# Scores from 16-bit pairs: rotated queries and keys of a two-layer decoder kept as two halves in 16 bits

## The chip, the cores and the metric

The kernel runs on one core of a Trainium2 chip. TensorE (PE in the profile) multiplies matrices into eight PSUM banks; VectorE (DVE), ScalarE (ACT) and GpSimd (POOL) work on tiles of 128 partitions in SBUF and on the banks; SyncE (SP) issues all DMA transfers. The metric is device time in microseconds, the median of the runs shown; lower is better.

## The reference, cut to what matters

Two decoder layers on x of 1024 tokens by 1024 features in float32. The part that the change touches is how scores of rotated queries and keys become softmax weights:

```
h = rms_norm(x, attn_norm[layer])
q, k = apply_rope(h @ Wq, cos, sin), apply_rope(h @ Wk, cos, sin)     # heads of 64 features
s = einsum(q, k) * 64**-0.5                                            # float32, masked
p = exp(s - max(s)) ; o = (p @ v) / sum(p)
```

Layer 0 has 8 heads of sparse attention, each in three branches (over compressed keys, selected blocks and a window of 512) and 8 heads with a window of 128 and a sink; with 1024 tokens the selected blocks are all blocks, so that branch is causal attention. Layer 1 has 16 heads of three dilated windows. After each attention comes an output projection, and after that a gated feed-forward block of 2816 hidden units.

## The kernel before, in words

**Numbers.** No large 32-bit product is made in one piece. An operand x is split into a high half h (x rounded to a shorter type) and a low half l = x - h, and a product is hh + lh + hl, three matmuls. Feed-forward weights and activations are split into two float16 halves under a power of two (lines 553 to 635, `splits`, `high`, `lows`). Projections, and rotated queries and keys, use the 32-bit type fp32r: the halves of a projection weight are two such tiles, and so are those of q and k.

**Where q and k come from.** `rope_job` (line 929) multiplies a group of four heads, `evac` takes the two banks out with the cosine and sine tables, and `fin` subtracts and adds the two parts, copies the result to a high tile on ACT, subtracts it from the result on DVE or POOL (`vg` chooses, line 412), and stores both tiles to DRAM with four DMAs. `apart` writes a second copy with every fourth token together for layer 1's far branch. `bk_job` does the same for one pair of keys. Compressed keys come from `cmp_tail`.

**Scores.** A branch loads its q and k (`load_q`, `load_k`, lines 1469 and 1479) as stacks: the 128 contraction rows are 64 features of the high and 64 of the low half of k, against the high half of q twice; a second matmul of 65 or 66 rows adds the high half of k times the low half of q and a row that subtracts the maximum. `s_issue` makes scores with the tokens on the partitions into a bank pS, `maxima` takes row maxima on DVE, TensorE transposes them, ACT copies them and a DMA writes them into that row. `st_unit` makes the transposed scores into a bank pT, at most 512 columns a unit; DVE adds masks, ACT takes the exponential (`weights`), the weights are split into two float16 halves, and `pv_unit` multiplies them with V into pO. In layer 1's second half a head has a far branch (G: two units of eight matmuls of 128 columns) and a near one (N).

**Order.** Five stages of dense jobs (projections, output projections, feed-forward, of one half of the tokens at a time) run in a fixed sequence; the attention of one half runs beside the dense jobs of another. At build time a list scheduler (`run`, line 377) simulates the engines with its own table of costs (`account`, line 295) and puts the instructions of all tasks into one fixed order per engine; on the chip each engine follows its order and waits on semaphores. A task may issue once a tile of its arena is free: S4 has 36 tiles of 4 KB per partition, S2 has 17 of 2 KB. Nearly all instructions are issued through one wrapper, so the profile shows them at one line, L242, and is read by tiles.

Of the kernel before, what the change touches and what calls it, by code (L numbers as in the profile page):

```python
# [10 lines left out]
F32 = mybir.dt.float32  # L11
# [24 lines left out]
FLOOR = -1.0e20  # L36
# [7 lines left out]
N4 = 36  # L44
N2 = 17
# [105 lines left out]
class W:  # L151


    def __init__(self, load, views=None):
        self.load, self.views = load, views
        self.st = self.h = self.l = None
        self.ok = self.split_ = False

# [100 lines left out]
class Kernel:  # L259
    def __init__(self, nc, tc, ctx, io):  # L260
# [15 lines left out]
        self.MR = arena("MR", 20, [P, HB], F32R)  # L276
        self.SM = arena("SM", NSM, [P, 8], F32)
        self.NM = arena("NM", 3, [HB, P], F32R)
# [16 lines left out]
    def account(self, key, name, a, kw):  # L295
# [14 lines left out]
        if key == "s":  # L310
            n = int(np.prod(a[0].shape)) * 4
# [108 lines left out]
    def constants(self):  # L420
# [10 lines left out]
        nc.vector.memset(self.ones, 1.0)  # L431
        self.onesR = c.tile([P, 2], F32R, name="onesr", tag="onesr")
# [13 lines left out]
    def more_constants(self):  # L446
# [8 lines left out]
        yield "v"  # L455
        nc.vector.tensor_scalar(self.sinks8, self.sinks, 1.0 / SCALE, None, op0=ALU.mult)
# [18 lines left out]
    def rows(self):  # L475
        nc = self.nc
        zero, one = self.S4.take(F32), self.S4.take(F32)
        nc.gpsimd.memset(zero.w[0:16], 0.0)
        nc.gpsimd.memset(one.w[0:16], -1.0)
        kh, ql = self.s0["k"][0], self.s0["q"][1]  # L480
        for r in range(2):
            yield "s"
            for i in (0, 4):
                self.dma(ql.some(i, 4)[64 + r], zero.w[0:4])
            for k0, set_ in ((0, r == 0), (2, r == 1), (4, r == 0)):
                if k0 < 4 or r == 0:
                    yield "s"
                    self.dma(kh.some(k0, 2)[64 + r], (one if set_ else zero).w[0:2])
        yield "s"
        for i in range(0, 16, 4):  # L490
            self.dma(self.s1["k"][0].some(i, 4)[64], one.w[0:4])
            self.dma(self.s4["k"][0].some(i, 4)[64], one.w[0:4])
        zero.drop()
        one.drop()
# [58 lines left out]
    def splits(self):  # L553
        for i, w in enumerate(self.wreq):
# [21 lines left out]
            else:  # L576
                w.l = self.S4.take()
                for h, l, s in w.parts():
                    self.nc.scalar.copy(h, s)
                w.split_ = True  # L580
            self.wsp = i + 1

# [346 lines left out]
    def rope_job(self, wt, cols_, n, h, outs, again=None):  # L929
# [4 lines left out]
        def run(*ws):  # L934
# [24 lines left out]
            def fin(kind, dst, head, a, b):  # L959
# [14 lines left out]
                store(dst, head, hb, lb)  # L974
# [3 lines left out]
            def store(dst, head, hb, lb):  # L978
                for z in range(2):
                    for d, b in zip(dst, (hb, lb)):  # L980
                        self.dma(d.some(head, 4)[z * 32:(z + 1) * 32, :, cs].rearrange("c h t -> (c h) t"), f(b.x[:, z]))
                hb.drop()
                lb.drop()
# [1728 lines left out]
```

## Time and profile before

| | |
|---|---|
| Median of three runs | 2691.47 us (2690.44 to 2698.56) |
| The profiled execution's own time | 2696.28 us |
| Span from its first to its last instruction | 2694.6 us |
| TensorE busy | 2548.9 us, 95% of the span |
| DVE, ACT, POOL busy | 1906.2, 1377.9, 779.2 us |
| Mean granted TensorE clock | 0.97 |
| DMA | 394.55 MB, 146 GB/s on average |

Busy time is when an instruction of the engine is running; for TensorE the ends of matmuls are modelled, so a cost per matmul is better read from one start to the next. In the names of tiles S is SBUF (both arenas), PH a tile of softmax weights, pS, pT, pO and pD are PSUM banks (scores for maxima, transposed scores, outputs of attention, dense products), MR row maxima, NM their transposed copy, SM small columns.

### The profile page before, as it was taken

The page shows a single profiled execution, that of the slowest core. Times are in us where ns is not written, and L with a number is a line of the kernel's source. Part 1 is how long each engine was busy: PE and PEld are TensorE (multiplying, and loading weights), DVE is VectorE, ACT ScalarE, POOL GpSimd, SP SyncE. Part 2 cuts the span into 40 slices and gives each one's busy share as a digit, 9 for nine tenths or more (in the row PEclk, how much of TensorE's full clock was granted, in tenths as well). Part 3 has the DMA queues.
Part 4 walks back from the last instruction along what each step waited for, and adds up shares of the span by engine and source line. Part 5 has one row for each costly group of instructions (what it writes and reads, how often), then busy time and mean ns, then how long its engine had stood idle before and what let it go on. Part 6 is the DMA issues. An engine that isn't in the chain of part 4 may idle for free. (4 is left out here: it accounts for less than half of the span.)

```text
span 2694.6 us, 42662 instructions
## 1 busy us (share of the span) xinstructions
PE 2548.9 (95%) x15462; PEld 1691.7 (63%) x15462; DVE 1906.2 (71%) x4270; ACT 1377.9 (51%) x2338; POOL 779.2 (29%) x538
## 2 busy tenths in 40 slices
PE   8878889999999999999999998998999999999998
PEld 7667668655555687765555687775555557754445
DVE  6988877877778776586666577677668885655554
ACT  6455545666666564353444465444556665443332
POOL 4545534211111347650000346533001114500002
PEclk9989989999999999999999999988899999999999
DMA  8655575333343245854444456995547664633320
GB/s 232 214 153 136 153 228 163 87 91 91 87 105 102 91 145 193 258 145 118 114 122 122 126 172 201 281 248 144 144 132 185 172 156 139 193 110 102 102 71 32
DMA packets 457367, 394.55 MB, mean 146 GB/s; under 512 B 53990, under 2 KB 383654, under 8 KB 457156
## 3 DMA queue, kind: packets, MB, share of 16 engines
q1 hardware_dynamic: 457156, 391.82, 50.9%
q8 instruction: 122, 2.00, 0.3%
q14 instruction: 89, 0.73, 0.1%
HBM read 311.43 MB, written 75.85 MB: 144 GB/s over the span
## 5 line engine op out<-in xcount | busy, mean ns | idle before, releaser
L242 PE MATMUL pD<-S,S 128*128 128x512 f16 (+3 forms) x9648 | 2180.7, 379 | 16.3 <-DVE S L242 11.4
L242 PEld LDWEIGHTS <-S 128*128 128x128 f16 x5376 | 511.4, 100 | 585.1 <-issue 35.6
L242 PEld LDWEIGHTS pD<-S,S 128*128 128x128 f32 x4272 | 734.5, 193 | 142.2 <-DVE S L242 8.8
L242 POOL TENSOR_TENSOR S<-S,S 128x1024 fp32r<-128x1024 f32 (+3 forms) x304 | 565.6, 1877 | 817.0 <-ACT S L242 662.1
L242 ACT CAST S<-S 128x512 fp32r<-128x512 f32 (+2 forms) x307 | 298.8, 1027 | 165.6 <-DVE S L242 72.8
L242 DVE SCALAR_TENSOR_TENSOR S<-S,wsc,S 128x1024 f16<-128x1024 f32 x224 | 295.3, 1319 | 60.8 <-ACT S L242 58.0
L242 ACT ACTIVATE S<-pT 128x512 f32<-128x512 f32 (+3 forms) x304 | 170.7, 565 | 297.9 <-DVE pT L242 252.6
L242 ACT ACTIVATE S<-S 128x1024 f16<-128x1024 f32 (+3 forms) x267 | 210.0, 787 | 158.4 <-DVE S L242 149.1
L242 ACT ACTIVATE S<-S,wsc 128x1024 f16<-128x1024 f32 x224 | 253.2, 1142 | 55.7 <-DVE wsc L242 50.0
L242 DVE TENSOR_TENSOR S<-S,S 128x512 fp32r<-128x512 f32 (+4 forms) x162 | 224.2, 1395 | 70.9 <-ACT S L242 63.7
L242 DVE SCALAR_TENSOR_TENSOR S<-pD,SM,S 128x512 f32<-128x512 f32 x208 | 156.2, 751 | 153.0 <-PE pD L242 143.6
L242 PE MATMUL pT<-S,S 128*128 128x128 f32 (+11 forms) x1072 | 226.0, 337 | 16.0 <-ACT S L242 12.9
L242 DVE TENSOR_TENSOR S<-pD,S 128x512 f32<-128x512 f32 (+1 forms) x238 | 156.7, 666 | 111.9 <-PE pD L242 96.5
L242 DVE TENSOR_TENSOR PH<-S,PH 128x512 f16<-128x512 f32 (+2 forms) x236 | 186.7, 796 | 39.8 <-ACT PH L242 37.9
L242 POOL TENSOR_TENSOR PH<-S,PH 128x512 f16<-128x512 f32 (+3 forms) x68 | 83.3, 1225 | 453.7 <-ACT PH L242 388.4
L242 PEld LDWEIGHTS pT<-S,S 128*128 128x128 f32 (+2 forms) x1072 | 173.2, 200 | 44.6 <-ACT S L242 18.0
L242 ACT ACTIVATE S<-pD,SM 128x512 f32<-128x512 f32 (+2 forms) x136 | 80.6, 604 | 210.6 <-PE pD L242 185.7
L242 ACT CAST PH<-S 128x512 f16<-128x512 f32 (+3 forms) x304 | 176.6, 588 | 13.4 <-PE pO L242 6.7
L242 PEld LDWEIGHTS <-PH 128*128 128x128 f16 (+1 forms) x3384 | 128.5, 101 | 72.6 <-DVE PH L242 24.7
L242 PE MATMUL pO<-S,PH 128*128 128x65 f16 (+1 forms) x3192 | 138.7, 199 | 27.9 <-DVE PH L242 20.8
L242 PE MATMUL pS<-S,S 128*128 128x256 f32 (+4 forms) x460 | 121.3, 352 | 20.4 <-DVE SM L242 12.2
L242 DVE TENSOR_TENSOR pT<-pT,S 128x128 f32<-128x128 f32 (+4 forms) x176 | 91.1, 523 | 50.9 <-PE pT L242 49.3
(175 smaller groups left out, 1798.4 us busy)
## 6 DMA issues: line engine op xcount, KB each, us to landing
S<-in_w_gate_up SPq DMA_DIRECT2D x176, 512.0 KB
S<-in_w_down SPq DMA_DIRECT2D x88, 512.0 KB
S<-in_w_qkv_o SPq DMA_DIRECT2D x48, 512.0 KB
S<-in_w_in_e SPq DMA_DIRECT2D x22, 512.0 KB
xd<-S SPq DMA_DIRECT2D x32, 256.0 KB
S<-dhq SPq DMA_DIRECT2D x64, 128.0 KB
S<-in_w_out_e SPq DMA_DIRECT2D x16, 512.0 KB
S<-xd SPq DMA_DIRECT2D x32, 256.0 KB
```

The lines of the kernel that those rows point to most:

```text
L242: return fn(*a, **kw)
```

## The change

Rotated queries and keys become float16 pairs under a power of two. The power comes from a bound: by Cauchy and Schwarz a projected column is no longer than the norm of the weights times sqrt(1024) times the norm's gain, so ACT squares the projection weights with a running sum (27 tiles, the first time each is loaded), TensorE sums over partitions, and four small DVE operations turn the sum into a power of two (`limited`, `power`). Halves then are h = f16(s x) and l = f16(s x - h), the second always on DVE. The scores carry the product of two such scales, which `joint` turns into factors for the exponential, the sinks and the mask tables; row maxima are kept divided by 32768 in float16. DRAM copies of q and k, the loads, and the tiles are 16-bit: q takes one S2 tile where it took an S4 tile, k one tile where it took two. S4 falls to 33 tiles and S2 rises to 22. The planner's rules stay as they are, with the new types in their place.

```diff
-N4 = 36
-N2 = 17
+N4 = 33
+N2 = 22
...
-        self.MR = arena("MR", 20, [P, HB], F32R)
+        self.MR = arena("MR", 20, [P, HB], F16)
...  splits()
+                if w.limit is not None:
...
+                    self.nc.scalar.activation(w.l.w, f(w.st.w), AF.Square, accum_out=k["acc"].t[:, k["i"]:k["i"] + 1])
+                    k["i"] += 1
+                    if k["i"] == k["n"]:
+                        self.go(self.limited(k), 2)
...
+    def limited(self, k):
+        nc, n = self.nc, k["n"]
+        ps = yield from self.over(k["acc"], n)
+        out, inv = k["t"][:, 0:1], k["t"][:, 1:2]
...
+        nc.vector.tensor_mul(out, out, self.long[k["layer"]])
+        self.power(out, out, inv)
+        self.have[("scale", id(k))] = self.scope
...
+    def joint(self, name, q, k):
...
+        nc.vector.scalar_tensor_tensor(t[:, 0:1], q["t"][:, 1:2], SCALE, k["t"][:, 1:2], op0=ALU.mult, op1=ALU.mult)
+        nc.vector.tensor_scalar(t[:, 1:2], t[:, 0:1], STEP, None, op0=ALU.mult)
+        nc.vector.tensor_scalar(t[:, 2:3], t[:, 0:1], -STEP, None, op0=ALU.mult)
+        nc.vector.tensor_mul(t[:, 3:4], q["t"][:, 0:1], k["t"][:, 0:1])
...  rope_job(), fin()
-                yield "a", self.room(S4=2)
-                hb, lb = self.S4.take(), self.S4.take()
-                nc.scalar.copy(hb.w, f(a.w))
-                yield "vg"
-                self.vg(1024, self.o.slack).tensor_sub(lb.w, f(a.w), f(hb.w))
+                yield "a", lambda: max(self.S4.when(), self.have.get(("scale", id(lim)), INF))
+                t = self.S4.take()
...
+                nc.scalar.activation(t.f16(1024), f(a.w), AF.Copy, scale=lim["s"])
+                yield "v"
+                nc.vector.scalar_tensor_tensor(t.f16(2048)[:, 1024:2048], f(a.w), lim["s"], t.f16(1024), op0=ALU.mult,
+                                               op1=ALU.subtract)
...  load_q(), load_k()
-        t = self.S4.take()
+        t = self.S2.take()
...
-            t = [self.S4.take(), self.S4.take()]
-            k1, k2 = t[0].w, t[1].w
+        t = (self.S4 if h else self.S2).take()
+        k1, k2 = self.kviews(t)
...  maxima()
-        nc.tensor.transpose(ps.t[0:HB, 0:P], m, self.ident)
+        nc.tensor.matmul(ps.t[0:HB, 0:P], br["m"].t, self.ident16, start=True, stop=True)
...  weights()
-            nc.vector.tensor_tensor(v, v, tab, op=ALU.add)
+            if br["kind"] in "CG":
+                nc.vector.scalar_tensor_tensor(v, tab, br["joint"][:, 3:4], v, op0=ALU.mult, op1=ALU.add)
+            else:
+                nc.vector.tensor_tensor(v, v, tab, op=ALU.add)
...
-        nc.scalar.activation(p.t[0:kp, 0:w], st.t[0:kp, 0:w], AF.Exp, scale=SCALE)
+        nc.scalar.activation(p.t[0:kp, 0:w], st.t[0:kp, 0:w], AF.Exp, scale=br["joint"][0:kp, 0:1])
...  whole()
-        heads = lambda name, c: Heads(lambda i, n: dr(f"{name}{i}", [66, n, T]), c)
+        heads = lambda name, c: Heads(lambda i, n: dr(f"{name}{i}", [66, n, T], F16), c)
```

Two places of the order show what moves. The first is on TensorE, in the second half of layer 1's attention, at a unit of a far branch (pT is its bank; the two S tiles behind the first are the two stacks of k, the S ahead of them q). Before:

```order
L242 MATMUL pS_23786<-ident,MR_23715 4x128
L242 LDWEIGHTS S_1287_23464
L242 MATMUL pD_23746<-S_1251_22651,S_1287_23464 128x512
...
L242 MATMUL pT_23801<-S_1270_23102,S_1271_23106 128x128
L242 MATMUL pT_23801<-S_1270_23102,S_1272_23107 128x128
```

And such a unit now:

```order
L245 LDWEIGHTS S_1076_22933
L245 MATMUL pT_23602<-S_591_22929,S_1076_22933 128x128
...
L245 MATMUL pS_23614<-SM_23589,ones 128x1
L245 LDWEIGHTS S_1091_23336
L245 MATMUL pD_23591<-S_989_20995,S_1091_23336 128x512
```

A 32-bit matmul brings its weights along in one instruction; a 16-bit one has a weight load of its own ahead of it, and both stacks of k now lie in one tile. The places of the units among the dense products stay nearly where they were.

The second is the low half of the rotated queries of layer 0's heads 4 to 7 in the first half. Before, on POOL (S_107 is the rotated result, S_117 its high half, S_118 its low half; S_115 is a plain query's low half; PH is a tile of softmax weights):

```order
L242 TENSOR_TENSOR S_107_1380<-S_107_1380,S_108_1381 128x512 x2
L242 TENSOR_TENSOR S_115_1484<-S_109_1423,S_114_1483 128x1024
L242 TENSOR_TENSOR S_118_1533<-S_107_1380,S_117_1532 128x1024
L242 TENSOR_TENSOR PH_1576<-S_38_1574,PH_1575 128x512
L242 TENSOR_TENSOR S_35_1406<-OS_1590,SM_1592 128x4x64
```

Now, on DVE (S_90 is the rotated result, `limq_200` its scale, S_100 the tile of both halves; the ISA rows are row maxima, the rows on pT are masks):

```order
L245 ISA junk,SM_1843<-pS_1865,mB 128x256
L245 ISA SM_1843 128x1
L245 SCALAR_TENSOR_TENSOR S_100_1811<-S_90_1583,limq_200,S_100_1811 128x1024
L245 TENSOR_TENSOR S_107_1884<-S_101_1844,S_106_1883 128x1024
L245 TENSOR_TENSOR pT_1889<-pT_1889,tDE 128x512
L245 TENSOR_TENSOR pT_1894<-pT_1894,tDE 128x256
```

The subtraction has left POOL's queue and stands in DVE's, between a row maximum and the masks.

## Rows read from the trace of the kernel before

**Rows 1.** This is the profile's part 1: busy time of each engine, its share of the span, and its instructions.

```profile
PE 2548.9 (95%) x15462; PEld 1691.7 (63%) x15462; DVE 1906.2 (71%) x4270; ACT 1377.9 (51%) x2338; POOL 779.2 (29%) x538
```

**Rows 2.** This is stretches of the whole program (from:to and length in us, then busy us and instructions of PE, its weight loads PEld, DVE, ACT and POOL, then the granted clock of TensorE, the DMA share and GB/s).

```profile
100.00:500.00 400.00, 341.31 (x2393) 275.76 (x2391) 340.67 (x813) 215.32 (x417) 189.81 (x129) 0.92 0.59 167
500.00:900.00 400.00, 397.91 (x2762) 229.29 (x2762) 312.34 (x846) 255.05 (x437) 58.01 (x53) 0.99 0.32 88
...
1700.00:1950.00 250.00, 220.70 (x1274) 159.99 (x1273) 169.60 (x437) 121.46 (x212) 70.88 (x52) 0.88 0.74 199
1950.00:2250.00 300.00, 298.08 (x1966) 171.70 (x1965) 229.50 (x673) 179.02 (x316) 44.35 (x41) 1.00 0.57 151
```

**Rows 3.** This is what TensorE waited for in the stretch from 100 to 500 us: us in total, times, longest; the first row of the view.

```profile
PE pS L242 <- DVE SM L242: 16.2, 12, 2.6
```

**Rows 4.** This is TensorE in order of time, in layer 1's second half (start in us, length with the pipeline's latency, operands and shape of the first of the merged instructions, how many). A group's cost is read from its start to the next row's start.

```profile
2100.38 5.34 PE L242 MATMUL pD<-S,S 128*128 128x512 f16 x24
2105.55 0.28 PE L242 MATMUL pS<-SM,ones 128*128 128x1 f32 x2
...
2112.05 0.90 PE L242 MATMUL pO<-S,PH 128*128 128x65 f16 x24
2112.79 0.27 PE L242 MATMUL pS<-ident,MR 128*4 128x128 f32 x1
2112.90 0.81 PE L242 MATMUL pD<-S,S 128*128 128x512 f16 x3
2113.36 1.20 PE L242 MATMUL pT<-S,S 128*128 128x128 f32 x8
2114.40 6.00 PE L242 MATMUL pD<-S,S 128*128 128x512 f16 x27
```

**Rows 5.** This is TensorE's groups with the shapes kept apart, of the whole span (stationary rows*columns, moving shape and type, count, then busy us, mean ns of one, and idle before them). pT takes the transposed scores, pS the scores for the maxima and the transposes of the row maxima (MR).

```profile
L242 PE MATMUL pT<-S,S 128*128 128x128 f32 x240 | 62.2, 282 | 4.4 <-ACT S L242 4.4
L242 PE MATMUL pS<-S,S 128*128 128x256 f32 x224 | 53.7, 329 | 13.8 <-DVE SM L242 6.2 <-DMA S<-glk 4.3 <-ACT NM L242 1.8
L242 PE MATMUL pT<-S,S 65*128 65x128 f32 x200 | 53.0, 292 | 0.0
L242 PE MATMUL pT<-S,S 128*128 128x256 f32 x152 | 51.6, 353 | 5.5 <-ACT S L242 3.4 <-DMA S<-in_w_in_e 2.1
L242 PE MATMUL pS<-S,S 128*128 128x512 f32 x104 | 47.5, 478 | 3.5 <-DVE SM L242 3.2 <-DVE wsc L242 0.3
L242 PE MATMUL pT<-S,S 128*128 128x512 f32 x88 | 46.2, 525 | 0.9 <-ACT S L242 0.9
L242 PE MATMUL pS<-ident,MR 128*4 128x128 f32 x112 | 32.3, 288 | 20.4 <-DVE MR L242 16.2 <-DVE SM L242 2.9 <-DVE wsc L242 0.4
L242 PE MATMUL pT<-S,S 65*128 65x256 f32 x112 | 30.7, 288 | 0.0
L242 PE MATMUL pS<-S,S 128*128 128x128 f32 x80 | 16.1, 250 | 0.2 <-DVE SM L242 0.2
L242 PE MATMUL pT<-S,S 66*128 66x128 f32 x40 | 11.2, 281 | 0.0
L242 PE MATMUL pS<-kc,S 128*128 128x64 f32 x64 | 9.4, 272 | 0.6 <-DMA S<-dhp 0.6
```

**Rows 6.** This is TensorE in order of time, in layer 0's second half, columns as in group 4.

```profile
602.43 1.46 PE L242 MATMUL pD<-S,S 128*128 128x512 f16 x6
603.53 0.82 PE L242 MATMUL pT<-S,S 128*128 128x512 f32 x2
604.19 0.64 PE L242 MATMUL pS<-S,S 128*128 128x512 f32 x2
...
615.09 3.41 PE L242 MATMUL pD<-S,S 128*128 128x512 f16 x15
618.15 0.83 PE L242 MATMUL pT<-S,S 128*128 128x256 f32 x4
618.82 0.28 PE L242 MATMUL pS<-SM,ones 128*128 128x1 f32 x2
```

**Rows 7.** This is the same view as group 2, for the instructions on the banks pT alone (first two rows) and pS alone (last two); the `sum` rows are over all nine stretches of the program.

```profile
100.00:500.00 400.00, 59.47 (x290) 46.83 (x290) 45.55 (x112) 48.20 (x89) 0.92 0.59 167
sum 2695.00, PE 244.28 PEld 182.49 DVE 163.32 ACT 181.15; mean PE 27.14 PEld 20.28 DVE 18.15 ACT 20.13
...
100.00:500.00 400.00, 62.58 (x286) 40.85 (x284) 71.71 (x161) 18.86 (x59) 0.92 0.59 167
sum 2695.00, PE 246.04 PEld 175.76 DVE 270.59 ACT 61.35; mean PE 27.34 PEld 19.53 DVE 30.07 ACT 6.82
```

**Rows 8.** This is groups of DVE, ACT and POOL with the shapes kept apart (count, then busy us, mean ns of one, idle before them). `wsc` and `gains` are scale factors; fp32r is the type of the high and low parts.

```profile
L242 DVE SCALAR_TENSOR_TENSOR S<-S,wsc,S 128x1024 f16<-128x1024 f32 x224 | 295.3, 1319 | 60.8 <-ACT S L242 58.0
L242 DVE TENSOR_TENSOR S<-S,S 128x512 fp32r<-128x512 f32 x69 | 98.3, 1437 | 51.3 <-ACT S L242 47.4 <-POOL S L242 3.4 <-issue 0.3
L242 DVE TENSOR_SCALAR wsc<-wsc 128x1 int32<-128x1 int32 x336 | 51.6, 154 | 11.6
L242 ACT ACTIVATE S<-S 128x1024 f16<-128x1024 f32 x112 | 117.4, 1048 | 8.5 <-PE pD L242 6.7 <-DMA S<-in_w_gate_up 1.6
L242 POOL TENSOR_TENSOR S<-S,S 128x1024 fp32r<-128x1024 f32 x93 | 234.1, 2522 | 132.1 <-ACT S L242 105.8 <-DMA S<-dlq 11.1 <-DMA S<-chk 7.8
```

More of the change, by code (lines that the diff above doesn't have):

```diff
@@ L454, in more_constants @@
             self.dma(g, src.rearrange("(k p) -> p k", p=P))
-        yield "v"
-        nc.vector.tensor_scalar(self.sinks8, self.sinks, 1.0 / SCALE, None, op0=ALU.mult)
+        for i in (0, 1):
+            yield "a", lambda i=i: max(self.SM.when(), self.est(self.gains[i]))
+            acc, junk = self.SM.take(), self.SM.take()
+            nc.scalar.activation(junk.t, self.gains[i], AF.Square, accum_out=acc.t[:, 0:1])
+            junk.drop()
+            ps = yield from self.over(acc, 1)
+            nc.vector.tensor_scalar(self.long[i], ps.t[:, 0:1], float(D), None, op0=ALU.mult)
+            ps.drop()
+            self.have["long", i] = self.scope
         for i in (2, 3):
@@ L1010, in rope_job @@
         n.uses += 2
-        return Job(48 * MM, run, self.rope_ws(wt, cols_))
+        lim, new = self.scale_of(name, layer, 2)
+        ws = self.rope_ws(wt, cols_)
+        for w in ws:
+            w.limit = new
+        return Job(48 * MM, run, ws)
     def used(self, n):
@@ L1068, in bk_job @@
         n.pairs = True
-        return Job(24 * MM, run, [W(load, views)])
+        lim, new = self.scale_of("kb", 0, 1)
+        wq = W(load, views)
+        wq.limit = new
+        return Job(24 * MM, run, [wq])
     def gemm_v(self, acc, n, b, w):
@@ L1965, in band, with both @@
         return g
+    def both(self, cond, *keys):
+        return lambda: max(cond(), self.known(*keys)())
     def known(self, *keys):
@@ L2000, in branches0 @@
             kv = i // 4
[L2001 removed]
+            j = ("joint", f"B{kv * 4}")
+            brs.append(dict(kind="B", joint=self.joints[j[1]], ok=self.both(ok(("q", 8 + i // 4 * 4), ("k", 4)), j), vok=vok(2), q=q[8 + i], k=kb[kv], row=0,
                             back=1, kparts=P, maskS=lambda: self.mB, maskT=self.band(1), v=vt(2, kv), vscale=sc(2),
@@ L2539, in whole @@
         self.wsc, self.wscn, self.scales = self.const.tile([P, 2 * NW16], F32, name="wsc", tag="wsc"), 0, {}
+        self.long = [self.const.tile([P, 1], F32, name=f"long{i}", tag=f"long{i}") for i in range(2)]
+        self.limits = {"c": dict(t=self.const.tile([P, 2], F32, tag="limc", name="limc"))}
         self.constants()
@@ L2575, in proj0 @@
                     outs.append(("plain", self.s0["p"], 4 * g))
-                jobs.append(self.rope_job(W0, [c0 + 64 * i for i in range(4)], n, h, outs))
+                jobs.append(self.rope_job(W0, [c0 + 64 * i for i in range(4)], n, h, outs, f"q{g}", 0))
             return jobs
```

233 lines of the change are left out of this document (144 added, 89 removed).

## The prediction, made before any run of the change

> **What bounds the kernel now.** I read the profile's first part, then a table of stages, then TensorE in order of time. TensorE is busy 95% of the span, VectorE (DVE) 71%, ScalarE (ACT) 51%, GpSimd (POOL) 29% [rows 1]: the reader is to see one engine nearly full and three with room. The stages refine it [rows 2]. From 500 to 900 us and from 1950 to 2250 us TensorE is busy 99% at a granted clock of 0.99 and 1.00: whatever is taken from its work there comes off the end. From 100 to 500 us it is busy 341 of 400 us, DVE 340.67 of 400 (85%), and the granted clock is 0.92, so part of the time it runs at 1.2 and not at 2.4 GHz. Here attention and projections alternate, TensorE stops between them, mostly until DVE has taken row maxima out of a score bank [rows 3], and the lower clock follows such stops. The stage from 1700 to 1950 us is of that kind too, but DVE has 32% to spare. DMA engines are busy 32 to 74% and no row makes them the bound.
>
> **Prices on TensorE, by start to next start.** A 16-bit 128x512 matmul costs (2105.55-2100.38)/24 = 0.2154 us [rows 4]. The eight 128-column score matmuls stand with three of those between 2112.90 and 2114.40: (1.50-3x0.2154)/8 = 0.1067 us each, for a quarter of the columns; a quarter of 0.2154 is 0.0539. By the same reading [rows 6], two 512-column scores cost (604.19-602.43-6x0.2154)/2 = 0.2338 each, four 256-column ones (618.82-615.09-15x0.2154)/4 = 0.1248 each, against 0.1077 for half of 0.2154. So the present type costs little where the moving side is wide, and about double where it is 128 wide.
>
> What does a 16-bit matmul with 128 columns and a weight load of its own cost? No row shows it. Below, the nearest is the product with V: 24 of them, 65 or 64 columns, each with its own weight load, take 2112.79-2112.05 = 0.74 us, 0.031 each [rows 4]. Above, it is the present 0.1067 (no gain). I take 0.0539, in proportion to the columns, because 0.031 for 65 columns is in proportion as well (0.027), so the 16-bit weight load hides even under 65 columns.
>
> **What is removed on TensorE.** 560 matmuls of 128 columns (240+200+40+80 [rows 5]) at 0.1067-0.0539 = 0.0528 give 29.6 us. 488 of 256 columns (224+152+112 [rows 5]) at 0.0171 give 8.3. 192 of 512 columns (104+88 [rows 5]) at 0.0184 give 3.5. The 64 matmuls against compressed keys (64 columns) are charged 0.1067 now and 0.031 then: 4.9. The 112 transposes of row maxima cost 2112.90-2112.79 = 0.11 [rows 4, 5] and become 16-bit products of 128 columns: 112 x 0.056 = 6.3. Together **52.6 us** at full clock.
>
> Of the work on the score banks, (59.47+62.58)/(244.28+246.04) = 25% lies in the stage from 100 to 500 us [rows 7]. So 13.1 us of the 52.6 fall where DVE is as busy as TensorE, and **39.5 us** fall elsewhere, nearly all under a full TensorE. I count those 39.5 in full.
>
> **What is added and moved.** The low half of a rotated q or k was a subtraction that the planner put on DVE or POOL; now it is a scaled subtraction that only DVE does. Layer 0 has 14 (ten rope jobs, four of them with a plain copy), all in the stage from 100 to 500 us or just ahead; layer 1 has 16, and 12 more of the strided copy in two halves. POOL paid 2.52 us for one, DVE will pay 1.32, the price of the same operation on the weights [rows 8]. In layer 0 that is 14 x 1.32 = 18.5 us more on DVE, where 59 us are free [rows 2]. The order shows such a split between a row maximum and the mask that the exponential waits for, so some of it comes through to TensorE. Bounds: nothing and 18.5; I take half, **+9.2**. In layer 1 it is 16 x 1.32 + 24 x 1.44 (the strided price [rows 8]) = 55.6 us at most; DVE is busy 68% in 1700 to 1950, so I cost it at nothing; were DVE full there, it would be 55.6.
>
> The bound needs 27 squares of weights on ACT at 1.05 us [rows 8] = 28 us, beside an engine that is busy 54 to 64% in these stages [rows 2], ahead of time since weights come several jobs early: nothing. About 120 one-column DVE operations at 0.154 [rows 8] = 19 us over the program: nothing outside the first stage. On TensorE, 17 more one- or two-column products and 14 more filler matmuls ahead of the first job, at the 0.11 of the short transpose [rows 4]: **+3.4**. Casts to fp32r become scaled casts to 16 bits on the same engine, same count: nothing. Q and K transfers halve in bytes, with as many issues on SP and half the buffers per branch; since no row waits long for them I give that nothing. The scaled mask additions on PSUM replace plain ones one for one: nothing.
>
> A rule speaks against my price. The Trainium skill ("TensorE: Matmul & The Clock Gate", Back-to-back issue gap) gives about 81 ns per matmul for streams of weight load and matmul at 128 columns in a real kernel. By that, an estimate from that page, 560 x 0.026 = 14.4 us would be saved and not 29.6. The 0.031 of the product with V speaks against it [rows 4]; no row has the 128-column case.
>
> **Sum.** -39.5 - 13.1 + 9.2 + 3.4 = -40.0 us. The profiled execution took 2696.28 us, which gives 2656.3; the median of the runs, 2691.47, is 4.8 below it, which gives **2651.5 us**.
>
> **Rivals.** (a) Stops shrink as well: the score chain gets shorter and half as many bytes come in, so some of the 400-341 = 59 us without TensorE in 100 to 500 us [rows 2] go, and fewer stretches run at the lower clock. If half goes and DVE costs nothing: 2651.5 - 9 - 29 = 2613. For it: 16.2 us of waits on a score bank alone [rows 3]. Against: these waits end with DVE, which gets more work.
> (b) The 16-bit matmul of 128 columns costs the middle of its bounds, 0.080: 560 x 0.027 = 15 us are saved there and not 29.6: 2666. The Trainium skill's section named above has nearly this number.
> (c) DVE becomes the bound from 100 to 500 us: the 13.1 are lost, all 18.5 come through and so do half of the small operations (9.5): -39.5+18.5+9.5+3.4 = -8 us, 2683, within the noise. It decides when DVE's busy share there goes past about 95%; the 18.5 bring it from 85 to 90%.
> (d) Slower: in both layers the splits sit in DVE's queue ahead of maxima, masks and PSUM evictions, and TensorE stops for each. Then 18.5+55.6+19+3.4 come on and 52.6 go off: +44, 2735. It needs DVE to have no slack in 1700 to 1950, against its 68%.
> (e) 16-bit scores cost TensorE what they do now: +3.4, 2695 at most. The 0.031 speaks against it; it would need weight loads that stay as long as in fp32r.
>
> **How the numbers follow.** A measurement of this kernel tells about 0.3% from no change, 8 us. Forecast 0.45, (a) 0.20, (b) 0.14, (c) 0.12, (d) 0.06, (e) 0.03. Faster by more than 8 us: forecast, (a), (b) and a little of (c), 0.81; same: the rest of (c) and (e), 0.13; slower: (d), 0.06. The range reaches from (a), with a few us for the clock, to (c): 2608 to 2687; beyond lie (d), (e) and the far end of (a).
>
> **What would show it.** In the changed profile the eight-matmul group of 128 columns should take about 0.43 us between its neighbours and not 0.85; the pT and pS banks together should fall from 490 us by 50 to 60; TensorE should stay above 98% from 500 to 900; DVE from 100 to 500 should rise from 85 to about 90%; POOL should lose about 28 of its 93 wide subtractions. I am wrong in the price if the 128-column group stays above 0.6 us, wrong in the cover if DVE passes 95% or TensorE's waits for DVE grow by more than 10 us, and wrong about the bound if TensorE's busy time falls by 50 us and the span doesn't.

## The result, and the profile after

The changed kernel takes 2657.74 us (median of 4 runs, 2656.5 to 2659.92); the kernel before, on the same chip, 2692.27 (2690.44 to 2698.56). The ratio is 0.9869, 95% interval 0.9851 to 0.9886: 34.5 us less, and 2651.5 had been forecast. The profiled execution took 2659.92 us, its span is 2658.1 (before: 2694.6).

Part 1 of its page, to be read against [rows 1]:

```profile
PE 2514.3 (95%) x15510; PEld 1586.3 (60%) x15510; DVE 1959.7 (74%) x4445; ACT 1437.0 (54%) x2398; POOL 720.1 (27%) x511
```

TensorE's busy time fell by 34.6 us and the span by 36.5, so the time in which TensorE stands idle is about what it was (145.7 us before, 143.8 now). The stages, with the columns of [rows 2]:

```profile
100.00:500.00 400.00, 348.13 (x2478) 253.73 (x2476) 353.26 (x868) 234.69 (x431) 196.03 (x139) 0.94 0.48 137
500.00:900.00 400.00, 391.34 (x2761) 206.09 (x2761) 316.64 (x866) 263.33 (x441) 58.16 (x52) 1.00 0.28 80
1700.00:1950.00 250.00, 235.03 (x1419) 157.03 (x1417) 199.23 (x489) 140.14 (x234) 71.06 (x50) 0.95 0.60 164
1950.00:2250.00 300.00, 298.08 (x2032) 171.15 (x2033) 236.81 (x665) 192.13 (x333) 66.64 (x54) 1.00 0.47 130
```

From 500 to 900 us TensorE is no longer full: 391.34 of 400 us and not 397.91. From 1700 to 1950 its clock went from 0.88 to 0.95. TensorE in order of time, in layer 1's second half (columns of [rows 4]):

```profile
2068.22 0.81 PE L245 MATMUL pD<-S,S 128*128 128x512 f16 x3
2068.96 0.22 PE L245 MATMUL pS<-ident,MR 128*4 128x128 f16 x1
2069.11 1.47 PE L245 MATMUL pD<-S,S 128*128 128x512 f16 x6
...
2084.11 0.63 PE L245 MATMUL pT<-S,S 128*128 128x128 f16 x8
2084.57 0.33 PE L245 MATMUL pS<-SM,ones 128*128 128x1 f32 x2
```

The eight 128-column scores take 2084.57-2084.11 = 0.46 us; 0.85 was read before, 0.43 forecast. But the product that turns maxima into rows, 0.11 us in [rows 4], begins 0.74 us after a group of three dense products that needs 3 x 0.2154 = 0.65, and lasts 0.15 to the next: 0.24 us where 0.054 was forecast.

Groups with the shapes kept apart (columns of [rows 5, 8]), and the sums of the banks pT and pS over nine stretches, as in [rows 7]:

```profile
L245 PE MATMUL pT<-S,S 128*128 128x128 f16 x240 | 41.4, 225 | 0.2 <-ACT S L245 0.2
L245 PE MATMUL pS<-ident,MR 128*4 128x128 f16 x112 | 24.8, 221 | 22.3 <-DVE MR L245 12.4 <-DVE SM L245 5.7 <-DVE vsc L245 1.2
L245 POOL TENSOR_TENSOR S<-S,S 128x1024 fp32r<-128x1024 f32 x65 | 162.0, 2494 | 101.8 <-ACT S L245 82.6 <-PE pT L245 8.6 <-DMA S<-dlk 8.4
```

```profile
sum 2658.00, PE 185.12 PEld 5.52 DVE 168.25 ACT 207.22; mean PE 20.57 PEld 0.61 DVE 18.69 ACT 23.02
sum 2658.00, PE 221.95 PEld 88.82 DVE 271.45 ACT 62.61; mean PE 24.66 PEld 9.87 DVE 30.16 ACT 6.96
```

The banks fell by 490.3 - 407.1 = 83 us, far more than the 34.6 of the engine. Rows of score products overlap those of their neighbours, so a bank's busy time is no measure of a saving; dense products' rows (9648 on pD) rose by 16 us meanwhile, from 2180.7 to 2196.5 us.

Where the time went is best seen by progress. This table, worked out from the traces, gives the time in us at which the n-th dense product (in units of 512 columns) starts, for the kernels below too:

```
                              300    1100    5000    5600    6000    7200     end
before                      103.0   491.5  1569.3  1739.5  1926.3  2246.7  2694.6
changed                     129.7   491.8  1578.7  1749.5  1888.9  2213.5  2658.1
e1 old buffers              127.4   519.3  1605.1  1770.2  2001.0  2290.1  2738.3
e2 no bound                 115.4   471.7  1556.2  1730.7  1866.5  2191.1  2636.1
e3 no bound, shared split   123.0   481.2  1562.0  1728.3  1852.6  2178.5  2623.2
e4 before, DVE splits       105.2   458.2  1532.5  1700.0  1863.9  2190.4  2637.4
e5 16 bits, old order       106.8   491.7  1565.3  1732.1  1906.9  2220.5  2668.2
e6 before, 35 and 18        107.7   498.5  1583.6  1747.3  1934.3  2254.8  2702.6
e7 changed, one spare       128.9   494.6  1578.3  1752.3  1889.2  2213.8  2658.5
e10 before, row 350         102.0   486.8  1561.4  1729.9  1914.8  2235.2  2683.2
e11 changed, full width     128.7   487.7  1567.0  1738.2  1874.9  2196.4  2641.1
e12 e4's order, 16 bits     102.7   456.3  1522.1  1689.6  1842.4  2160.4  2608.5
```

The changed kernel loses 26.7 us in the first 300 products, is level at the 1100th, is 10 behind at the 5600th, and then wins 47 within 400 products. That is not a price per product spread over full stages.

What goes there are stops of the dense products, counted from the start of the last dense product to the start of the next; those over 8 us are meant. Before, three of 18.3, 26.7 and 22.1 us begin between 1740 and 1890 us; the changed kernel has one of 20.5 us between 1690 and 2000 us. This is the first of the three, and then the one that is left (what ended a wait stands in brackets behind its length):

```profile
1743.69 2.71 PE L242 MATMUL pD<-S,S 128*128 128x512 f32 x11
1746.24 0.64 PE L242 MATMUL pS<-S,S 128*128 128x256 f32 x4
1749.36 0.27 PE L242 MATMUL pS<-ident,MR 128*4 128x128 f32 x1 [2.48 <-DVE MR L242]
...
1764.35 2.16 PE L242 MATMUL pD<-S,S 128*128 128x512 f32 x4
```

```profile
1799.27 1.64 PE L245 MATMUL pD<-S,S 128*128 128x512 f32 x6
1800.76 0.64 PE L245 MATMUL pT<-S,S 128*128 128x128 f16 x8
...
1821.04 1.83 PE L245 MATMUL pD<-S,S 128*128 128x512 f32 x3
```

In between TensorE works on attention alone, with waits. From the 5600th to the 6000th product the mean granted clock is 0.84 before and 0.90 now.

### The profile page after: what moved, and what is told of

It is laid out like the page before. It is cut to its first block, busy times and chain, and to the rows that moved or that the text cites. A ratio compares the mean times of both kernels' runs of the same rounds, so it can differ in the third digit from the quotient of the medians.

```text
span 2658.1 us, 42701 instructions
## 1 busy us (share of the span) xinstructions
PE 2514.3 (95%) x15510; PEld 1586.3 (60%) x15510; DVE 1959.7 (74%) x4445; ACT 1437.0 (54%) x2398; POOL 720.1 (27%) x511
## 4 chain that ended last, share of the span: by engine, by line
PE 42%; DVE 9%; issue 3%; ACT 2%; DMA 2%; POOL 1%; SPq 1%; DVEq 0%; POOLq 0%; ACTq 0%
PE pD L245 38%; DVE S L245 6%; PE pS L245 2%; ACT S L245 1%; PE pT L245 1%; PE pO L245 1%; DVE SM L245 1%; POOL S L245 1%; DVE pT L245 1%; DVE junk L245 1%; SPq L245 1%; DMA S<-in_w_out_o 1%; DMA S<-xd 0%; DVE PH L245 0%; DMA S<-in_w_out_e 0%
## 5 line engine op out<-in xcount | busy, mean ns | idle before, releaser
L245 PE MATMUL pD<-S,S 128*128 128x512 f16 (+3 forms) x9648 | 2196.5, 379 | 28.6 <-DVE S L245 23.7
L245 PEld LDWEIGHTS <-S 128*128 128x128 f16 (+2 forms) x6960 | 644.6, 100 | 712.4 <-issue 87.1
L245 POOL TENSOR_TENSOR S<-S,S 128x512 f32<-128x512 f32 (+3 forms) x261 | 480.2, 1853 | 819.8 <-ACT S L245 682.4
L245 ACT ACTIVATE S<-S 128x1024 f16<-128x1024 f32 (+4 forms) x294 | 238.1, 811 | 133.4 <-DVE S L245 131.8
L245 ACT CAST S<-S 128x512 fp32r<-128x512 f32 (+2 forms) x251 | 241.1, 1016 | 102.1 <-DVE S L245 59.0
L245 DVE TENSOR_TENSOR S<-S,S 128x512 fp32r<-128x512 f32 (+3 forms) x149 | 191.8, 1299 | 62.0 <-ACT S L245 58.0
L245 DVE TENSOR_TENSOR PH<-S,PH 128x512 f16<-128x512 f32 (+3 forms) x228 | 168.0, 741 | 43.1 <-ACT PH L245 42.0
L245 PE MATMUL pT<-S,S 128*128 128x128 f16 (+11 forms) x1072 | 167.3, 279 | 11.6 <-ACT S L245 8.3
L245 ACT ACTIVATE S<-pT,jointC 128x512 f32<-128x512 f32 (+1 forms) x112 | 73.2, 655 | 165.4 <-DVE pT L245 163.8
L245 ACT ACTIVATE S<-pT,jointA 128x512 f32<-128x512 f32 (+1 forms) x144 | 92.1, 648 | 116.0 <-DVE pT L245 87.6
L245 PE MATMUL pS<-S,S 128*128 128x256 f16 (+4 forms) x460 | 98.8, 302 | 20.4 <-DVE SM L245 14.9
```

What stands on the lines that cost most here:

```text
L245: return fn(*a, **kw)
```

## The experiments

**e1: the old buffers.** Queries again in an S4 tile, keys in one S4 tile in the first half and two in the second, rotation results in two. The edit, shortened:

```diff
-N4 = 33
-N2 = 22
+N4 = 35
+N2 = 18
...  rope_job(), fin()
-                t = self.S4.take()
+                t, t2 = self.S4.take(), self.S4.take()
...  load_q(), load_k()
-        t = self.S2.take()
+        t = self.S4.take()
...
-        t = (self.S4 if h else self.S2).take()
+        t = [self.S4.take() for _ in range(1 + h)]
```

> The changed kernel with the buffers of the kernel before: queries in an S4 buffer each, keys of the second half in two, rotation results in two, N4 = 35 and N2 = 18 (as many bytes as the change has). The arithmetic, the bound and the halved transfers stay. PRICE theory (the sum on record: the gain is cheaper score products and shorter stops, buffers are worth nothing): 2658, between 2652 and 2664, and in 1700 to 1950 us one stretch in which the dense products stop, as in the changed kernel. BUFFER theory (the gain of 35 us that falls between 1740 and 1930 us comes from S4 buffers that are free earlier, so that weights load and split in time): 2685 to 2693, with two or three stretches again in which only scores run at half the clock. ORDER theory (which stops there are is an accident of the order that the planner writes out): anywhere from 2645 to 2695, the stops at other places than in either kernel.

2744.57 us, ratio to before 1.0205 (1.0188 to 1.0223): 87 us over the changed kernel, beyond what any theory gave. By the table it is 27.5 us behind the changed kernel at the 1100th product, 26.4 at the 5000th, 112 at the 6000th and 80 at the end: two places. The first is a stop of the dense products from 198 to 286 us; this is the stretch (columns of [rows 2]), and what SP issued around it from the weights of projections (`in_w_in_e`) and of the compression (`in_cmp_k_w`):

```profile
198.00:286.00 88.00, 65.05 (x594) 40.04 (x593) 67.41 (x233) 53.95 (x116) 23.64 (x29) 0.69 0.14 37
```

```profile
184.80 0.44 SPq L245 DMA_DIRECT2D S<-in_w_in_e  x1
216.05 0.54 SPq L245 DMA_DIRECT2D S<-in_cmp_k_w  x1
289.87 0.58 SPq L245 DMA_DIRECT2D S<-in_cmp_k_w  x1
290.57 0.45 SPq L245 DMA_DIRECT2D S<-in_w_in_e  x1
```

For 105 us no projection weight is fetched, in the 88 us of the stop DMA is at 14%, and attention alone runs at a granted clock of 0.69. The second place is five stops between 1780 and 2038 us, 14.4, 11.4, 55.3, 22.2 and 13.6 us long, where the changed kernel has the one of 20.5. Weights live in S4 buffers, and so do queries, keys and rotated results here; that the weights lacked a buffer is read from the gap and the edit, and not shown row by row. The bound isn't what stops the dense products: the last sum that it needs for layer 0's projections is there at 144 us. So the smaller buffers are not worth nothing: the change needs them.

**e2: without the bound; e3: and with the split on DVE or POOL again.** Shortened, first what both have, then what e3 has besides:

```diff
...  splits()
-                if w.limit is not None:
+                if False:
...  scale_of()
+            self.nc.vector.memset(k["t"], 1.0)
+            self.have[("scale", id(k))] = 0.0
...  e3: rope_job(), fin()
-                yield "v"
-                nc.vector.scalar_tensor_tensor(t.f16(2048)[:, 1024:2048], f(a.w), lim["s"], t.f16(1024), op0=ALU.mult,
-                                               op1=ALU.subtract)
+                yield "vg"
+                self.vg(1024, self.o.slack).tensor_sub(t.f16(2048)[:, 1024:2048], f(a.w), t.f16(1024))
```

> The changed kernel without the bound: every scale is the constant 1, so the 27 ACT squares, the ones-products, the powers and the waits for them are gone; the 16-bit pairs and their splits on DVE stay. Left out is the finding of the bound (and one spare buffer fewer is kept ahead of the compression, which the planner needs to finish its order). PRICE theory: the bound cost 3.4 us, so 2654. START theory (the first 300 dense products end 26.7 us later than before because early products wait for the bound): the first 300 dense products end at least 15 us earlier than in the changed kernel; if nothing after it takes that back, 2631 to 2643. ORDER theory: 2640 to 2690, without relation to the start.

2644.14 us, ratio 0.9829 (0.9812 to 0.9846). The first 300 products end 14.3 us sooner, so START theory's 15 and 2643 are each missed by about a us.

> The kernel without the bound (every scale the constant 1), and the low halves of queries and keys made by a subtraction that the planner may put on DVE or POOL, as before the change, and not by DVE alone. PRICE theory: 9.2 us less than the kernel without the bound, that is 2645; between 100 and 500 us DVE falls from 88% to about 84%. If DVE splits cost nothing on the path: the same time as without the bound, within 5 us. ORDER theory: up to 20 us to either side of it.

2623.7 us, ratio 0.9754 (0.9738 to 0.977). DVE didn't fall to 84% between 100 and 500 us: it is at 88% in e2 and 89% in e3.

**e7** is the control for both: the changed kernel with their spare number.

```diff
-            yield "vg", lambda: max(self.S4.when(5, 2), self.est(zn))
+            yield "vg", lambda: max(self.S4.when(5, 1), self.est(zn))
```

> The changed kernel with the one number that the two kernels without the bound also have: the planner keeps one spare buffer and not two ahead of the compression. The same instructions, in another order in the first stage. If that number was worth nothing: 2658. If it explains the gain of the kernel without the bound: 2644. ORDER theory: 2640 to 2690.

2663.41 us, ratio 0.9891 (0.9874 to 0.9908): that number explains nothing of e2. Against e7 the bound costs 19 us by the medians, 22.4 by the spans, and by the table all of it before the 1100th product (22.9), with 13.5 in the first 300. Without the bound the planner also writes another order, so part of this can be order. The four longest waits of TensorE there on a bank pS, in the changed kernel up to 130 us, in order of time:

```profile
36.16 0.58 PE L245 MATMUL pS<-SM,ones 128*128 128x2 f32 x2 [5.60 <-ACT S L245]
39.46 0.58 PE L245 MATMUL pS<-SM,ones 128*128 128x1 f32 x2 [2.72 <-ACT SM L245]
70.00 0.27 PE L245 MATMUL pS<-ident,SM 128*3 128x128 f32 x1 [3.14 <-DVE SM L245]
124.35 0.59 PE L245 MATMUL pS<-S,S 128*128 128x256 f16 x2 [6.30 <-DVE SM L245]
```

The first two are ones-products of the bound, standing in TensorE's queue ahead of dense products: 8.3 us, gone in e2. The other two aren't products of the bound: one transposes small columns (0.81 us of wait in e2), one makes scores and waits for row maxima (no such wait in e2 up to 120 us). Against that, one wait of dense products for DVE (`gates`) grows in e2 from 2.4 to 7.9. Up to the 300th product the granted clock is 0.88 in e7 and 0.95 in e2. e3 is 20 us below e2 by the medians (12.9 by the spans), but not where the forecast had put it: it is 9.5 behind e2 at the 1100th product and wins after the 5000th.

**e4: the kernel before, low halves on DVE alone.** One of three places of the edit:

```diff
-                yield "vg"
-                self.vg(1024, self.o.slack).tensor_sub(lb.w, f(a.w), f(hb.w))
+                yield "v"
+                nc.vector.tensor_sub(lb.w, f(a.w), f(hb.w))
```

> The kernel before with one edit: the low halves of queries and keys, which the planner puts on DVE or POOL, all on DVE (32-bit, as before). PRICE theory: half of 14 times 1.32 us comes through in layer 0 and nothing in layer 1, so 2692 + 9 = 2701. Rival (d) of the prediction: the splits stop TensorE in both layers, some 70 us, 2760. If they hide altogether: 2692. ORDER theory: 2675 to 2710, with the stops between 1740 and 1930 us at other places.

2640.16 us, ratio 0.982 (0.9804 to 0.9835): 50 us less than before, from putting all these splits on the busier engine. Theories that price the split are out, with either sign: here sharing costs, between e2 and e3 it gains. The edit lets the planner write another order; what in that order is better was not taken apart.

**e5: 16-bit pairs in the old order.** No bound, no new buffers, the planner told the old prices, so every engine keeps its order instruction by instruction (but for one copy of the identity). Three of its places:

```diff
-                nc.scalar.copy(hb.w, f(a.w))
+                nc.scalar.copy(hb.f16(1024), f(a.w))
...
-        nc.tensor.transpose(ps.t[0:HB, 0:P], m, self.ident)
+        nc.tensor.matmul(ps.t[0:HB, 0:P], br["m"].t, self.ident16, start=True, stop=True)
...
-        heads = lambda name, c: Heads(lambda i, n: dr(f"{name}{i}", [66, n, T]), c)
+        heads = lambda name, c: Heads(lambda i, n: dr(f"{name}{i}", [66, n, T], F16), c)
```

> The kernel before with 16-bit pairs and nothing else: queries, keys, compressed keys, maxima and their rows are 16-bit floats in DRAM, in SBUF and in the products, unscaled; no bound, the buffers of before, the splits on DVE or POOL as before, and the planner is told the old prices of products and bytes, so that every engine but for one added 16-bit copy of the identity matrix has the order of before, instruction by instruction. PRICE theory (sum on record without its splits and bound): 2692 less 52.6 for the products, and some stops shorter, so 2640 or less. ORDER theory (the savings that rows of one score product show are partly charged to its neighbours: over 1339 dense 16-bit products in full stretches the scores' rows fell by 28 us, the dense products' rows grew by 20, so 8 us are real of 28): 0.28 of 52.6, 15 us, so 2677, and the three stops between 1740 and 1930 us are all there.

2665.62 us, ratio 0.9906 (0.9891 to 0.9921): cheaper products and half the bytes are worth 25 us, not 53 and not 15. The three long stops of the stage are all there, with the same products in them, 16.8, 23.9 and 17.1 us long where before they were 18.3, 26.7 and 22.1. Part 1 of the page:

```profile
PE 2514.6 (94%) x15462; PEld 1588.0 (60%) x15462; DVE 1898.2 (71%) x4271; ACT 1376.0 (52%) x2338; POOL 768.2 (29%) x538
```

Busy time falls by 34.3 us, the span by 26.4: 7.9 us come back as idle time. What TensorE waits for over the span, e5 and then the kernel before:

```profile
PE pS L242 <- DVE SM L242: 32.1, 29, 3.8
PE pS L242 <- DVE MR L242: 20.0, 24, 4.1
...
PE pT L242 <- ACT S L242: 18.2, 13, 2.5
```

```profile
PE pS L242 <- DVE SM L242: 29.2, 24, 3.1
...
PE pS L242 <- DVE MR L242: 16.2, 18, 4.0
PE pT L242 <- ACT S L242: 13.8, 12, 2.5
```

TensorE comes sooner to maxima and exponentials that DVE and ACT make at their old pace. By the table 12.0 of the 26.4 us are won between the 5600th and the 6000th product, where the stops are and the granted clock went from 0.84 to 0.86, and 4.2 between the 1100th and the 5000th, where TensorE is full.

**e6 and e10: another order, the same arithmetic.** The kernel before with `N4 = 35`, `N2 = 18`, and with `rowlat=350.0` for `300.0`.

> The kernel before with one S4 buffer fewer and one S2 buffer more (N4 = 35, N2 = 18); the same instructions, in another order wherever the planner meets a shortage. BUFFER theory: slower than before by 5 to 30 us, in the stretches with stops (150 to 470 and 1740 to 1930 us). ORDER theory: any time from 2640 to 2745; whatever differs lies in those two stretches, and between the 1100th and the 5000th dense product the time is the same within 3 us.

2702.8 us, ratio 1.0039 (1.0024 to 1.0055).

> The kernel before with one number of the planner changed: it believes that a row of maxima lands 350 ns and not 300 ns after its transfer is written. The same instructions, buffers and arithmetic, some of them in another place. ORDER theory: a change of 5 to 40 us in either direction, all of it in the first 1100 and the 5000th to 7200th dense product, with stops at other places. If an order without a cause in the arithmetic is worth nothing: 2691 within 5 us.

2683.73 us, ratio 0.997 (0.9956 to 0.9983). Against the kernel before on the same chip these are +12 us (2690.83) and -9 (2692.45). Only e10 is neutral: e6 takes an S4 buffer away, and its BUFFER theory, 5 to 30 us slower, holds as well as ORDER does. It isn't all in the two places: e6 loses another 7.3 between the 1100th and the 5000th product, e10 gains 3.2.

**e8 and e9: TensorE alone.** Periods of four dense products and a group.

> None of the computation: TensorE alone, under its full clock, in six stretches of 30 periods of four dense 16-bit products (128x512, 0.2155 us each, 0.862 us) and a group of score pairs, 32-bit or 16-bit; then 30 periods of the four and one four-column transposing product; then pairs alone. PRICE theory, by rows of single groups: eight 128-column products cost 0.854 us more per period at 32 bits and 0.431 at 16, four 256-column ones 0.499 and 0.431, two 512-column ones 0.468 and 0.431, a transposing product 0.11 and 0.054. NEIGHBOUR theory (the row of a 32-bit product begins while the dense product ahead of it still runs, or the dense product behind a 16-bit one waits for its weights): the difference per period is under half of that, 0.12 us for the eight and under 0.04 for the others, while the rows of single products show the forecast's prices.

> None of the computation: TensorE alone under its full clock, in periods of four dense 16-bit products (0.861 us) and one more product of 128 moving columns. In the first such kernel the 32-bit transposing product of four stationary columns cost 0.111 us a period and the 16-bit one that the change uses 0.256, so that the change loses 112 times 0.145 = 16 us there. Here the 16-bit product has 4, 16, 32, 64 and 128 stationary columns, is a transpose into a 16-bit bank, stands twice in a row, and a 32-bit rounded product has 4. If 16 bits themselves are dear in this place: 0.25 at every width. If the narrow weights are: 0.06 to 0.11 from some width on, and the 32-bit rounded one with 4 columns may be as dear as the 16-bit one. Besides, groups of four products of 64 moving columns, 32-bit and 16-bit: by the forecast 0.077 us apart each.

In order of time: eight 128-column products at 32 bits and at 16 stand between the rows of each pair.

```profile
120.48 1.04 PE L48 MATMUL bD<-m,w 128*128 128x512 f16 x4
121.17 0.41 PE L54 MATMUL bA<-q,k 128*128 128x128 f32 x1
...
122.21 1.04 PE L48 MATMUL bD<-m,w 128*128 128x512 f16 x4
...
180.95 1.03 PE L48 MATMUL bD<-m,w 128*128 128x512 f16 x4
181.82 0.22 PE L54 MATMUL bB<-q,k 128*128 128x128 f16 x1
...
182.28 1.03 PE L48 MATMUL bD<-m,w 128*128 128x512 f16 x4
```

Periods of 1.73 and 1.33 us, less 0.861 for the four: 0.108 a product at 32 bits, 0.059 at 16. The row of the first 32-bit product begins 0.69 us into the period, before the four can have been worked off: that is the overlap of the rows. The turn of the maxima in e9, with 4 and with 128 stationary columns:

```profile
150.45 1.04 PE L48 MATMUL bD<-m,w 128*128 128x512 f16 x4
151.42 0.22 PE L61 MATMUL bE<-id,r 128*4 128x128 f16 x1
151.57 1.04 PE L48 MATMUL bD<-m,w 128*128 128x512 f16 x4
...
312.38 1.03 PE L48 MATMUL bD<-m,w 128*128 128x512 f16 x4
313.24 0.22 PE L63 MATMUL bG<-id,k 128*128 128x128 f16 x1
313.30 1.03 PE L48 MATMUL bD<-m,w 128*128 128x512 f16 x4
```

1.12 us and 0.92. All medians of some 29 periods, less 0.861, per product:

```
                              32 bits   16 bits   forecast (32, 16)
128 columns, pairs of scores   0.108     0.059     0.1067, 0.0539
256 columns                    0.124     0.112     0.1248, 0.1077
512 columns                    0.239     0.219     0.2338, 0.2154
64 columns                     0.096     0.030     0.1067, 0.031
turn of the maxima             0.111     0.256     0.11,   0.054
  16, 32, 64 stationary columns          0.262, 0.269, 0.282
  128 stationary columns                 0.058
```

The score prices were right. The turn was not: at 16 bits it is dear at every width from 4 to 64, and cheap at 128. (In e9 a 16-bit transpose of 4 columns into a 16-bit bank costs 0.256 as well, and a product of the type fp32r with 4 columns 0.076.) With the forecast's counts the prices give 27.8 + 5.9 + 3.8 + 4.3 - 16.2 = 25.6 us; that e5 measured 25.2 is partly chance. The forecast's counts leave out 152 scores of 384 columns, 88 of 512 and 40 of 256 (second products of 65 or 66 rows) and 32 of 512 against compressed keys; idle time came back; and the places differ. By these prices and the trace's counts about 10 us should come between the 1100th and the 5000th product and 5 between the 5600th and the 6000th, where e5 won 4.2 and 12.0. The NEIGHBOUR theory falls for prices (the period shows 397 ns less, not 120); the overlap of rows it spoke of is real.

**e11: the changed kernel at full width.** The same order on every engine but for one swap of neighbours on DVE. Three places of the edit, the compressed keys, the maxima and the turn:

```diff
-                t = self.const.tile([P, 2, 64], F16, name=f"kc{hh}", tag=f"kc{hh}")
+                t = self.const.tile([P, 2, P], F16, name=f"kc{hh}", tag=f"kc{hh}")
...
-        nc.vector.tensor_scalar(br["m"].t, top, br["sink"][1] if "sink" in br else FLOOR, 1.0 / STEP, op0=ALU.max,
+        top = top[:, None, :].to_broadcast([P, P // HB, HB])
+        nc.vector.tensor_scalar(br["m"].raw.rearrange("p (r b) -> p r b", b=HB), top, br["sink"][1] if "sink" in br else FLOOR, 1.0 / STEP, op0=ALU.max,
...
-        nc.tensor.matmul(ps.t[0:HB, 0:P], br["m"].t, self.ident16, start=True, stop=True)
+        nc.tensor.matmul(ps.t[:, 0:P], br["m"].raw, self.ident16, start=True, stop=True)
```

> The changed kernel, every engine in its order instruction by instruction, with full-width weights in two places: DVE writes the four maxima 32 times over, so that the product that turns them into rows has 128 stationary columns and not 4, and the compressed keys have 128 columns and not 64 where they are stationary. Both are 16-bit as in the change. From the two kernels of TensorE alone: a turn with 4 columns cost 0.256 us a period and one with 128 columns 0.058, so 112 turns give back 22 us; the 32 products with compressed keys, by the rise of the 64-column row over the 128-column one (0.282 to 0.058), up to 7 us more. WIDTH theory: 2658 less 22 to 29, 2629 to 2636. If the turns mostly stand in stops, where TensorE waits for other engines anyway: 2645 to 2655. If the probes don't carry over: 2658.

2645.26 us, ratio 0.9833 (0.9811 to 0.9855): 12.5 less than the changed kernel by the medians, 17.0 by the spans. Part 1 and one turn:

```profile
PE 2487.5 (94%) x15510; PEld 1583.0 (60%) x15510; DVE 1963.1 (74%) x4445; ACT 1436.8 (54%) x2398; POOL 723.8 (27%) x511
```

```profile
2052.02 0.81 PE L245 MATMUL pD<-S,S 128*128 128x512 f16 x3
2052.66 0.22 PE L245 MATMUL pS<-ident,MR 128*128 128x128 f16 x1
2052.72 1.46 PE L245 MATMUL pD<-S,S 128*128 128x512 f16 x6
```

The turn now costs 0.06 us, and busy time falls by 26.8 us, as the probes said (22 to 29, of which 22 for the turns and the rest for the compressed keys; the two weren't run apart). The span keeps 17.0 of it; 9.8 return as idle time.

**e12: order and price together**, e4's order with e5's arithmetic and e11's wide turn.

> The kernel before in the order of the kernel with all low halves on DVE (2640 us), and in that order 16-bit pairs without bound (as in the kernel that kept the old order) and 128 stationary columns for the product that turns the maxima into rows. PRICE and ORDER are two separate terms: by the probes the products give 560 times 0.0496, 488 times 0.012, 192 times 0.020, 64 times 0.067 and 112 times 0.053, that is 27.8 + 5.9 + 3.8 + 4.3 + 5.9 = 47.7 us, of which the 32 products with 64 stationary compressed keys take back up to 7; so 2593 to 2600. If the order gives nothing more once products are cheap (TensorE was waiting for other engines in what is left of stops): 2610 to 2640. If the turns stay dear at full width: 2615.

2609.9 us, ratio 0.97 (0.9679 to 0.972), the fastest here, without the bound. Part 1:

```profile
PE 2477.0 (95%) x15462; PEld 1571.6 (60%) x15462; DVE 1920.8 (74%) x4303; ACT 1378.2 (53%) x2340; POOL 695.6 (27%) x504
```

e4's TensorE was busy 2518.4 us, so 41.4 are taken off (41 to 48 expected), and the span falls by 28.9. Price and order both count, but they don't add in full: 2593 to 2600 is missed by 10 us, and the time lies at the edge of the theory by which the order gives nothing more (2610 to 2640). A good quarter of the price comes back as idle time, as in e5 and e11.

## Why the number was right and the sum was not

The forecast missed by 6 us and its range held, through errors that cancel; that is luck.

1. **The price of scores** was right to within 6% at 128 columns (0.0496 saved, 0.0528 forecast), the term that carried the sum. Rival (b) is out: 0.059 against its 0.080. The Trainium skill ("TensorE: Matmul & The Clock Gate", Back-to-back issue gap) has about 81 ns for such a stream; these runs do not agree. Rival (e) is out by the same row. The forecast's counts left scores out (see e8 and e9), some 2 us at the prices measured besides the 384-column ones, which no run priced.
2. **"The 112 transposes ... become 16-bit products of 128 columns: 112 x 0.056 = 6.3"** failed. It priced by the moving columns. With 4 stationary columns the turn rose from 0.111 to 0.256, 16 us lost, a swing of 22.5 in the sum; e11, with the compressed keys, gave 12 to 17 back.
3. **"I count those 39.5 in full"** failed. Of the busy time saved, 23% (7.9 of 34.3), 37% (9.8 of 26.8) and 30% (12.5 of 41.4) came back as idle time in e5, e11 and e12, and from the 1100th to the 5000th product, where TensorE was full, e5 won 4.2 us. From 500 to 900 us TensorE fell to 97.8% in the changed kernel, under the 98% named; in the old order (e5) it stayed at 99.0%, so that fall isn't the price's alone. With 2, the products gave 25 and not 52.6.
4. **The bound at 3.4** was too low: about 19 us. The working priced the ones-products and not their place: two of them wait 8.3 us for squares on ACT in front of the dense products of the first stage, and the granted clock up to the 300th product is 0.88 with the bound and 0.95 without. The rest of the 19 wasn't taken apart; part of it can be order.
5. **Splits at +9.2** have no support. POOL lost just the 28 wide subtractions forecast (93 to 65), DVE rose to 88% of 100 to 500 us, short of 90, and rival (c) didn't come. TensorE's waits for DVE over the span stayed (91.6 us before, 90.5 after), so the sign of a wrong cover didn't show either. But e4, which moves the 32-bit splits to DVE, gained 50 us, against rival (d), and e3 gained 20 from undoing the move: the planner wrote another order for each of them.
6. **"Half the buffers per branch ... I give that nothing"** failed: undone in the changed kernel, it costs 87 us. From the 5600th to the 6000th product the changed kernel and e2, e3, e7, e11, all with small buffers, take 124 to 139 us; before and e1, e4, e5, e6, e10, e12, with large ones, 153 to 231. This is where the 47 us are won that carry the result. But small buffers aren't a gain by themselves. e12 has no bound, 16-bit pairs and the splits on DVE as e2 has, and large buffers in e4's order; it takes 2609.9 us and e2 2644.14. Without the full width, which gave 12 to 17 us in e11, e12 would be at 2622 to 2627 (an estimate), still under e2.

The change is then -25 for the products (e5), +19 for the bound (e2 against e7), and about -28 left over for buffers, splits and the order that they bring (-34.5 + 25 - 19). That remainder is a difference, not a measurement. e1 shows that the changed kernel needs its buffers, and e10 that some 9 us can be the planner's accident. Open: how it divides between buffers and order, and why e4's order is so much better. The 50 us of e4 are more than the whole remainder, so the splits on DVE could make it up by their order alone; no run holds the order and changes the buffers, to tell the two apart.

Rival (a) was right that stops go, and wrong in the reason, a shorter chain. It named the stage from 100 to 500 us: there the 300th to the 1100th product take 362 us and not 388, and the longest stop there is 8.4 us and not 27.8. With cheaper products alone (e5) it is 26.7 us, and the three of 1740 to 1930 us go from 67 to 58 together and none is gone. And "mostly until DVE has taken row maxima out" was too much for that stage: [rows 3] is 16.2 of the 56.5 us that TensorE waited there.

## What to carry to other kernels

Price a narrower type by both operands, stationary and moving, and in a stream, period against period; rows of one bank overlap their neighbours. Don't count what is saved on the full engine in full: here about a quarter to over a third of it came back as waits for the other engines. Where a planner writes the order, run the new arithmetic once in the old order and the old arithmetic once in a neutral new one, before a difference of 1% is given a cause; and ask of buffers who else draws on the pool: when queries and keys took back their S4 buffers (e1), no projection weight was fetched for 105 us and the dense products stopped.

## What was not expected of the hardware

A 16-bit product with 4, 16, 32 or 64 stationary columns cost 0.256 to 0.282 us among full-width products, with 128 columns 0.058, and two such products of 4 columns in a row 0.312 together: the second adds 0.056, so the cost lies in going from full width to narrow and back (the product's row begins 0.106 us after the four dense products should be worked off, and the next dense one 0.150 after that), hardly in the product itself. The 32-bit transposing product with the same 4 columns cost 0.111. And a row may begin before the engine gets to its product: the 32-bit one began 0.69 us into a period whose dense products take 0.861.

The prediction has the lower clock follow stops of TensorE. At the end of e8 score pairs stand alone, and TensorE is busy without a break. With 32-bit pairs, from 485.8 us on, the granted clock still fell: it is 1.00 up to 491.9 us and 0.50 from there to 525, and a product took 0.113 us and then 0.213. With the 16-bit pairs, from 542.7 to 556.7 us, it stayed at 1.00, and a product took 0.058. That isn't a rule for 16-bit scores: in the stop of e1, where they wait for other engines, the clock was 0.69.
